# A diffusion block's second feed-forward network: first-matrix tiles in pairs of seven half-size products, mixed with the second matrix in eighths

## The chip, the core and the metric

The kernel runs on one core of a Trainium2 chip. The metric is device microseconds of an execution; the time before is the median of three runs. The engines are TensorE (PE, with its weight loads as PEld), VectorE (DVE), ScalarE (ACT), GpSimd (POOL) and SyncE (SP), which issues the transfers.

## What is computed

Two layers of a transformer block over 512 latent tokens of width 1024 (and 256 context tokens in layer 0): attention, LayerNorm, a squared-ReLU network of width 4096, LayerNorm. The change is in the network of layer 1:

```python
def sqrelu_mlp(h, w1, w2):
    return jnp.square(jax.nn.relu(h @ w1)) @ w2

x = layer_norm(alpha * x + g1 * ax, ln1_g[i], ln1_b[i])
fx = sqrelu_mlp(x * (1.0 + sc2) + sh2, mlp_w1[i], mlp_w2[i])
x = layer_norm(alpha * x + g2 * fx, ln2_g[i], ln2_b[i])
```

All is float32. A product is made of three passes: each operand is split in a high part (rounded to float32r) and the rest, and high x high, high x low and low x high are summed in PSUM.

## The kernel before

*Products and splits.* `mm3` (L321 to L324) issues the three matmuls of 128 x 128 x n. `wsplit` (L297 to L318) brings a 128 x 1024 weight tile: a transfer into `w_raw` (four buffers), the cast `w_h` on ScalarE (L264), the subtraction `w_l` on VectorE (L312). `w_h` and `w_l` have four buffers each (`NH`).

*The order.* TensorE's order is written out by generators that the class `Flow` runs with a planned clock: a `yield` names what must be done before the next matmuls are issued. The other engines' order is made by the framework's scheduler from the same program. Every engine works its queue in order.

*Layer 1's network, `mlp` with l = 1.* `ln_job` (L521 on) transposes a normalised token block of 128 on TensorE (`xn_t`, L532), ScalarE scales it into `hx_v` (two buffers that it shares with `g_tmp`), and two splits write `hx1m`. The hidden width has 32 tiles of 128. They are worked in four quarters of eight tiles: for each tile 8 x 3 matmuls of 512 columns (`h_ps`, a wide accumulator of which PSUM holds two; the weight is the stationary operand, the tokens stream), then `relu` on ScalarE, the square on GpSimd (in the first quarter on VectorE), the cast `hid` and its subtraction. Tiles 0 to 3 are done in two slices of 256 tokens, so that they can start before the last token blocks are ready. Then `tok_product` works the second matrix: for either half of the 1024 outputs and each of four token blocks a group of 24 matmuls of 512 columns (`y_ps`, one of four narrow accumulators), with four weight tiles for a half. The groups of quarter 0 are copied into `fx`, those of quarters 1 and 2 are added to it on VectorE; then `fx` is multiplied by the gate and added to `acc` on GpSimd. The last quarter goes straight through `gated_add` (L560 on): `g_tmp` on VectorE, the sum into `acc` (on GpSimd for half 0, on VectorE for half 1), the statistics `bn`.

*The end.* `done4` takes a block's moments, has GpSimd raise the variance to -1/2 (`rstd`), and VectorE does two passes of 1024 with `l2g` and `l2b`, then the block goes out. The last group of all is done in two slices of 256 outputs.

Of the kernel before, what the change touches and what calls it, by code (L numbers as in the profile page):

```python
# [234 lines left out]
def hybrid_block(ctx: ExitStack, tc: tile.TileContext, t: dict, out: bass.AP):  # L235
# [31 lines left out]
    def gp(us, deps, fn, lat=LAT, **kw):  # L267
        fn(**kw)  # L268
# [51 lines left out]

    def mm3(o, lh, ll, rh, rl, start, stop):  # L321
        nc.tensor.matmul(out=o, lhsT=lh, rhs=rh, start=start, stop=False)  # L322
        nc.tensor.matmul(out=o, lhsT=lh, rhs=rl, start=False, stop=False)  # L323
        last["pe"] = nc.tensor.matmul(out=o, lhsT=ll, rhs=rh, start=False, stop=stop)  # L324

# [194 lines left out]

    def ln_job(pool, acc, tb, hx, A, B, ready, st, dep):  # L521
        dep = normalise(acc, st, dep)
# [3 lines left out]
        for q in range(2):  # L526
            yield [dep, sm_.ok]
            pt = psm("xn_t")
            slot = sm_.take()
            for j in range(4):  # L530
                k = 4 * q + j
                nc.tensor.transpose(out=pt[:, j * P:(j + 1) * P], in_=acc[:, k * P:(k + 1) * P], identity=ident)  # L532
            p = fl.pe(4 * mm(128))
            v = pool.tile([P, 4, P], F32, name="hx_v", tag="tmp", bufs=2)
# [1148 lines left out]
```

## Time and profile before

| what | value |
| --- | --- |
| median of three runs | 1679.1 us (1677.09 to 1680.61) |
| span of the profiled execution | 1669.8 us |
| what lies around the span, by the median | 9.3 us |
| PE, PEld busy | 1609.0, 1387.8 us |
| DVE, ACT, POOL busy | 935.4, 669.1, 344.2 us |
| layer 1's network and the end | from 1297.5 us on |

The profile is one execution. A page gives busy time by engine, then the chain of work that ended last, then groups of instructions by line. A row of the timeline reads: start, duration, engine, line, operation, out<-in, shape, count, and in brackets the idle time before it with what ended it. Matmuls overlap, so a row's duration is more than its step: the time of a matmul in a row of them is the distance of starts. A row of a table by stretches reads: window, length, then busy time and count of PE, PEld, DVE, ACT and POOL, the granted clock of TensorE, the share of the transfer engines and their GB/s.

### The profile page before, as it was taken

To read this page: it belongs to the slowest core of one execution; us is meant where nothing else is said; L and a number is where in the kernel's file an instruction comes from. 1 tells how busy PE (TensorE), PEld (TensorE's weight loads), DVE (VectorE), ACT (ScalarE), POOL (GpSimd) and SP (SyncE) were. 2 spreads that over 40 slices of the span, in tenths; PEclk is the share of its full clock that TensorE was granted. 3 is DMA by queue.
4 is the path that set the end of the run, shared out by engine and by line. 5 is a ranking of instruction groups with operands and counts; after the bars stand their busy time and mean duration, and the time that the engine had idled before them with its cause. 6 is when DMAs were issued, how large, how long until landed. Compare 5 with 4: busy or idle time off the path is not lost.

```text
span 1669.8 us, 23525 instructions
## 1 busy us (share of the span) xinstructions
PE 1609.0 (96%) x9153; PEld 1387.8 (83%) x9153; DVE 935.4 (56%) x1717; ACT 669.1 (40%) x1377; POOL 344.2 (21%) x314
## 2 busy tenths in 40 slices
PE   7899999999999999999999999999989899999998
PEld 5787777789889889879978998999877888888886
DVE  4655677668845353344446777776757552332436
ACT  3465675363223113212316555555543533222231
POOL 1333454100002001342211122221000001113422
PEclk9999999999999999999999999999999999999999
DMA  9111550524443243344312122211133323232321
GB/s 371 41 51 33 178 177 28 195 81 160 142 161 127 88 147 131 101 126 139 114 54 101 51 71 72 66 45 39 48 114 116 105 94 105 73 115 76 114 89 51
DMA packets 57239, 174.77 MB, mean 105 GB/s; under 512 B 7144, under 2 KB 13096, under 8 KB 57128
## 3 DMA queue, kind: packets, MB, share of 16 engines
q1 hardware_dynamic: 57128, 173.27, 30.8%
q8 instruction: 72, 1.18, 0.3%
q14 instruction: 39, 0.32, 0.1%
HBM read 165.35 MB, written 7.90 MB: 104 GB/s over the span
## 4 chain that ended last, share of the span: by engine, by line
PE 76%; DVE 9%; issue 5%; ACT 4%; DMA 3%; POOL 3%; SPq 0%; DVEq 0%; POOLq 0%; ACTq 0%
PE y_ps L324 10%; PE y_ps L323 10%; PE y_ps L322 10%; PE h_ps L322 8%; PE h_ps L323 8%; PE h_ps L324 8%; PE qkv_ps L322 2%; PE qkv_ps L323 2%; PE qkv_ps L324 2%; PE o_ps L1060 2%; PE s_ps L1376 2%; PE pT_ps L1078 2%; DVE w_l L312 2%; PE o_ps L1414 1%; PE s_ps L1027 1%
## 5 line engine op out<-in xcount | busy, mean ns | idle before, releaser
L264 ACT CAST w_h<-w_raw 128x1024 fp32r<-128x1024 f32 (+1 forms) x185 | 186.6, 1015 | 406.6 <-PE y_ps L324 207.9
L312 DVE TENSOR_TENSOR w_l<-w_raw,w_h 128x1024 fp32r<-128x1024 f32 (+1 forms) x185 | 222.1, 1211 | 216.3 <-ACT w_h L264 215.9
L323 PE MATMUL y_ps<-w_l,hid 128*128 128x512 f32 (+1 forms) x648 | 254.2, 392 | 1.8 <-DVE w_l L312 1.7
L324 PE MATMUL y_ps<-w_h,hid 128*128 128x512 f32 (+1 forms) x648 | 254.2, 392 | 0.4 <-DVE hid L260 0.2
L322 PE MATMUL y_ps<-w_h,hid 128*128 128x512 f32 (+1 forms) x648 | 254.3, 392 | 0.0
L268 POOL TENSOR_TENSOR relu<-relu 128x768 f32<-128x768 f32 (+1 forms) x48 | 80.9, 1686 | 604.2 <-ACT relu L264 604.2
L324 PE MATMUL h_ps<-hx0m,w_l 128*128 128x384 f32 (+1 forms) x528 | 175.4, 332 | 1.2 <-DVE w_l L312 1.0
L322 PE MATMUL h_ps<-hx0m,w_h 128*128 128x384 f32 (+1 forms) x528 | 175.2, 332 | 0.0
L323 PE MATMUL h_ps<-hx0m,w_h 128*128 128x384 f32 (+1 forms) x528 | 174.9, 331 | 0.0
L323 PEld LDWEIGHTS y_ps<-w_l,hid 128*128 128x128 f32 x648 | 121.9, 188 | 30.9 <-DVE w_l L312 3.3
L324 PEld LDWEIGHTS y_ps<-w_h,hid 128*128 128x128 f32 x648 | 121.9, 188 | 29.5 <-DVE hid L260 1.8
L322 PEld LDWEIGHTS y_ps<-w_h,hid 128*128 128x128 f32 x648 | 122.0, 188 | 28.0
L322 PE MATMUL qkv_ps<-w_h,hx 128*128 128x384 f32 (+1 forms) x384 | 126.9, 331 | 0.1
L323 PE MATMUL qkv_ps<-w_l,hx 128*128 128x384 f32 (+1 forms) x384 | 122.4, 319 | 0.7 <-DVE w_l L312 0.7
L324 PE MATMUL qkv_ps<-w_h,hx 128*128 128x384 f32 (+1 forms) x384 | 122.1, 318 | 0.0
L268 POOL TENSOR_TENSOR e<-e,sm 128x512 f32<-128x512 f32 (+2 forms) x96 | 92.7, 978 | 109.7 <-DVE sm L260 90.5
L322 PE MATMUL h_ps<-hx1m,w_h 128*128 128x512 f32 (+1 forms) x288 | 107.7, 374 | 3.5 <-ACT relu L264 3.5
L323 PE MATMUL h_ps<-hx1m,w_h 128*128 128x512 f32 (+1 forms) x288 | 107.2, 372 | 0.0
L324 PE MATMUL h_ps<-hx1m,w_l 128*128 128x512 f32 (+1 forms) x288 | 107.1, 372 | 0.0
L324 PEld LDWEIGHTS h_ps<-hx0m,w_l 128*128 128x128 f32 x528 | 99.1, 188 | 2.4 <-DVE w_l L312 2.4
L322 PEld LDWEIGHTS h_ps<-hx0m,w_h 128*128 128x128 f32 x528 | 99.1, 188 | 0.2
L323 PEld LDWEIGHTS h_ps<-hx0m,w_h 128*128 128x128 f32 x528 | 99.1, 188 | 0.1
(226 smaller groups left out, 3092.3 us busy)
## 6 DMA issues: line engine op xcount, KB each, us to landing
w_raw<-in_w SPq DMA_DIRECT2D x128, 512.0 KB, 3.5
w_raw<-in_w_adaT SPq DMA_DIRECT2D x56, 512.0 KB, 3.5
w_raw<-in_w_ada SPq DMA_DIRECT2D x24, 512.0 KB, 4.4
w_raw<-in_b_w SPq DMA_DIRECT2D x32, 384.0 KB, 3.5
raw<-in_w_ada SPq DMA_DIRECT2D x16, 512.0 KB, 9.5
w_raw<-in_a_wq SPq DMA_DIRECT2D x8, 512.0 KB, 4.3
w_raw<-in_a_wo SPq DMA_DIRECT2D x8, 512.0 KB, 4.2
w_raw<-in_b_wo SPq DMA_DIRECT2D x8, 512.0 KB, 4.1
```

The lines of the kernel that those rows point to most:

```text
L264: fn(**kw)
L268: fn(**kw)
L312: last["split"] = nc.vector.tensor_tensor(**kw)
L322: nc.tensor.matmul(out=o, lhsT=lh, rhs=rh, start=start, stop=False)
L323: nc.tensor.matmul(out=o, lhsT=lh, rhs=rl, start=False, stop=False)
L324: last["pe"] = nc.tensor.matmul(out=o, lhsT=ll, rhs=rh, start=False, stop=stop)
L1027: nc.tensor.matmul(out=sp[:, 512:512 + CTX], lhsT=q_, rhs=kT[:, kvh, hl, SEQ:TOK], start=(hl == 0), stop=(hl == 1))
L1060: nc.tensor.matmul(out=po[odd * HD:odd * HD + HD, 0:256], lhsT=vv[:, kb, kvh], rhs=pt_[:, odd * 256:odd * 256 + 256], start=(i == 0), stop ...
L1078: nc.tensor.transpose(out=pp[:, c * P:(c + 1) * P], in_=es[j][:, i * P:(i + 1) * P], identity=ident)
L1376: nc.tensor.matmul(out=sp[:, c * 512:c * 512 + 384], lhsT=qTt[:, tt, hl, qb * P:(qb + 1) * P], rhs=kS[:, tt, c * 384:c * 384 + 384], start ...
L1414: nc.tensor.matmul(out=po[:, qp * 256:(qp + 1) * 256], lhsT=vt[:, kb, vl], rhs=pt_[:, pl, a * 256:a * 256 + 256], start=(kp == 0 and pl == ...
```

## The change

Layer 1's network gets a function of its own, `mlp_pipe`; layer 0 keeps `mlp`. In it:

- Hidden tiles 0 to 5 are done as before (`plain`).
- Tiles 6 to 31 are done in 13 pairs, q = 3 to 15. A pair and the tokens are cut in 2 x 2 blocks: A (two weight tiles by two halves of the inner 1024) and B (the halves of the inner 1024 by two halves of the tokens). By Strassen's method in Winograd's form seven products A11, A12, S2, S1, S3, A22, S4 of 4 x 3 matmuls of 256 columns give the four blocks for which eight were needed. GpSimd makes the sums of weight blocks (`part_sums`: `e3`, `e1`, `e2` and the last for S4); each of the seven is split into a tile `w_half` that holds both parts (four buffers).
- Sums and differences of token blocks are made once (`token_sums`: eight differences on GpSimd in place in `fx`, which keeps the transposed tokens, then splits into `T`).
- Three products sum up in one accumulator X: it is copied out by ScalarE (`a1`, `a2`, `a3`) before the next product adds to it. VectorE adds the other products from two narrow accumulators. ScalarE does relu and square.
- The second matrix goes in eighths: eight sets of 512 hidden values; a group is 12 matmuls of 512 columns (`y_half` twice), for half of the outputs and one token block, and `sink` sums into `fx`. Between the products of a pair four groups are put (`mix`), in pairs 14 and 15 four half groups. `ahead` asks for the next pair's first four half tiles and for two second-matrix tiles.
- `last_y` does what is left: two groups of the eighth 6 (half 1) left open in their accumulators, then the eighth 7: half 0, then half 1 with the open groups first; blocks 2 and 3 do both eighths' half 1.
- `bc` tiles have three buffers instead of four, `hx_v` is gone in layer 1.

The core of the diff:

```diff
-NRAW, NH = 3, 4
+NRAW, NH, NQ = 3, 4, 4
...
+    def mlp_pipe(l, hx, ready, apool, pool, late, ntok, acc, get_gates, done, res, fx, T):
...
+        def part_sums(q):
+            (a1, g1, f1), (a2, g2, f2) = raw_tile(), raw_tile()
...
+            yield half(a11, q1)
+            w12 = half(a12, q1)
+            yield w12
+            e3 = add(s3, a11, a21, ALU.subtract, [q1, q2])
+            e1 = add(a21, a21, a22, ALU.add, [e3])
+            e2 = add(s2, a21, a11, ALU.subtract, [e1])
+            yield half(s2, e2)
+            yield half(a21, e1)
+            yield half(s3, e3)
+            w = half(a22, q2)
...
+            w = half(a12, add(a12, a12, s2, ALU.subtract, [e2, w12.t]))
...
+        def product(o, w, b, start):
+            kw = {} if start else {"skip_group_check": True}
+            for kk in range(4):
+                c_ = slice(kk * P, (kk + 1) * P)
+                mm3(o, w.h[:, c_], w.l[:, c_], b(kk, 0), b(kk, 1), start and kk == 0, kk == 3, **kw)
...
+        def pair(q, mix, ahead):
...
+            p = product(X, A11, lower(t1, 0), True)
+            a1 = ac(nh, [p], nc.scalar.copy, out=r0[:, t1], in_=X)
...
+            p = product(y[:, 0:nh], A12, lower(t1, 4), True)
...
+            yield from mix()
+            yield [a1, S2.t, Tr[1]]
+            p = product(X, S2, whole(1), False)
+            a2 = ac(nh, [p], nc.scalar.copy, out=r0[:, t2], in_=X)
...
+            p5 = product(z, S1, whole(0), True)
+            yield from mix()
+            yield [a2, S3.t, Tr[2]]
+            p = product(X, S3, whole(2), False)
+            a3 = ac(nh, [p], nc.scalar.copy, out=r1[:, t2], in_=X)
+            d3 = dv(nh, [p5, a3], nc.vector.tensor_tensor, out=r1[:, t2], in0=z, in1=r1[:, t2], op=ALU.add)
+            ahead()
+            yield from mix()
+            yield [a3, A22.t, Tr[3]]
+            p = product(X, A22, whole(3), False)
...
+            yield [d3, S4.t]
+            p = product(z, S4, lower(t2, 4), False)
...
+            squared(q, 0, r0, [d], slice(0, ntok))
+            yield from mix()
...
+            early = []
+            y_weights(6, 1)
+            y_weights(7, 0)
...
+            y_weights(7, 1)
...
+        yield from plain(range(4), [slice(i, i + 256) for i in range(0, ntok, 256)], sums)
+        yield from plain((4, 5), [slice(0, ntok)])
...
+        for q in range(3, 16):
+            n = 2 if q < 14 else 1
...
+            yield from pair(q, steps(ys, n), ahead)
+        yield from steps(ys, 99)()
+        yield from last_y()
```

Three places of the built program. The first is ScalarE inside the network. Before, between tiles 2 and 4 of the second quarter, a weight tile's cast, a relu out of PSUM and a `hid` cast follow each other:

```order
L264 CAST w_h_13545<-w_raw_13544 128x1024 [waits DMAHW2_49,DVE_49,PE_49]
L264 ACTIVATE relu_13430<-h_ps_13399 128x512 [waits DVE_49,PE_49]
L264 CAST hid_13324<-relu_13430 128x512 [waits Pool_49]
L264 CAST w_h_13581<-w_raw_13580 128x1024 [waits DMAHW3_49,PE_49]
L264 ACTIVATE relu_13466<-h_ps_13435 128x512 [waits DVE_49,PE_49]
L264 CAST hid_13324<-relu_13466 128x512 [waits Pool_49]
```

Now, in pair 6 from its first product on (13732 is the accumulator X, 13733 and 13734 the two result tiles, 13721, 13724, 13728 the half tiles S3, A22, S4, 13835 the next pair's A11, 13857 the second weight tile of a later group):

```order
L264 CAST w_half_13721<-w_sum_13631 128x512 [waits PE_49]
L264 COPY relu_13733<-h_ps_13732 128x256
L264 CAST w_half_13724<-w_raw_13628 128x512 [waits PE_49]
L264 CAST w_h_13857<-w_raw_13856 128x1024 [waits DMAHW6_49]
L264 CAST w_half_13728<-w_raw_13627 128x512 [waits PE_49,Pool_49]
L264 COPY relu_13733<-h_ps_13732 128x256
L264 CAST w_half_13835<-w_raw_13830 128x512 [waits DMAHW4_49,DVE_49,PE_49]
L264 COPY relu_13734<-h_ps_13732 128x256 [waits DVE_49,PE_49]
L264 CAST w_half_13838<-w_raw_13830 128x512 [waits DVE_49]
L264 ACTIVATE relu_13734<-relu_13734 128x256 [waits DVE_49]
```

The copies of X, for which TensorE waits, stand behind casts of half tiles and, in one place, behind a cast that waits for a transfer.

The second is TensorE at the start of the last half of the second matrix. Before, the first group takes a new weight tile every six matmuls, four in all:

```order
L322 MATMUL y_ps_14897<-w_h_14874,hid_14437 128x512 [waits DVE_49,Activation_49]
L323 MATMUL y_ps_14897<-w_l_14875,hid_14437 128x512 [waits DVE_49]
L324 MATMUL y_ps_14897<-w_h_14874,hid_14437 128x512
L322 MATMUL y_ps_14897<-w_h_14874,hid_14437 128x512
L323 MATMUL y_ps_14897<-w_l_14875,hid_14437 128x512
L324 MATMUL y_ps_14897<-w_h_14874,hid_14437 128x512
L322 MATMUL y_ps_14897<-w_h_14880,hid_14438 128x512 [waits Activation_49]
```

Now it takes two (the eighth (7,1): 15792 and 15798, in the buffers in which (7,0) lay), and the accumulator 15693 holds the eighth 6 already:

```order
L325 MATMUL y_ps_15773<-w_l_15689,hid_15544 128x512
L326 MATMUL y_ps_15773<-w_h_15688,hid_15544 128x512
L324 MATMUL y_ps_15693<-w_h_15792,hid_15365 128x512 [waits Activation_49]
L325 MATMUL y_ps_15693<-w_l_15793,hid_15365 128x512 [waits DVE_49]
L326 MATMUL y_ps_15693<-w_h_15792,hid_15365 128x512
L324 MATMUL y_ps_15693<-w_h_15792,hid_15365 128x512
L325 MATMUL y_ps_15693<-w_l_15793,hid_15365 128x512
L326 MATMUL y_ps_15693<-w_h_15792,hid_15365 128x512
L324 MATMUL y_ps_15693<-w_h_15798,hid_15544 128x512 [waits Activation_49]
```

So the group that ends ahead of it is the one that frees the buffers of its weights.

The third is VectorE at the end, from block 2's product with its gate on (12407 is block 2, 12408 block 3). Before:

```order
L563 TENSOR_TENSOR g_tmp_15000<-y_ps_14975,g2x_14163 128x512 [waits PE_49]
L260 TENSOR_TENSOR acc1_12407<-acc1_12407,g_tmp_15000 128x512 [waits DVE_49]
L260 BN_STATS bn_14841<-acc1_12407 128x6 [waits DVE_49]
L260 BN_AGGR mv_15004<-bn_14841 128x2 [waits DVE_49]
L260 TENSOR_SCALAR rstd_15006<-mv_15004 128x1 [waits DVE_49]
L260 SCALAR_TENSOR_TENSOR acc1_12407<-acc1_12407,mv_15004,l2g_14926 128x1024
L260 TENSOR_TENSOR g_tmp_15037<-y_ps_15012,g2x_14163 128x256 [waits PE_49]
L260 SCALAR_TENSOR_TENSOR acc1_12407<-acc1_12407,rstd_15006,l2b_14928 128x1024 [waits DVE_49,Pool_49]
```

Now block 1's second wide pass (12406) stands behind block 2's first row:

```order
L568 TENSOR_TENSOR g_tmp_15880<-y_ps_15855,g2x_14533 128x512 [waits PE_49]
L260 SCALAR_TENSOR_TENSOR acc1_12406<-acc1_12406,rstd_15849,l2b_15821 128x1024 [waits DVE_49,Pool_49]
L260 TENSOR_TENSOR acc1_12407<-acc1_12407,g_tmp_15880 128x512 [waits DVE_49]
L260 BN_STATS bn_15771<-acc1_12407 128x6 [waits DVE_49]
L260 TENSOR_TENSOR g_tmp_15917<-y_ps_15892,g2x_14533 128x256 [waits PE_49]
L260 BN_AGGR mv_15884<-bn_15771 128x2 [waits DVE_49]
L260 TENSOR_TENSOR acc1_12408<-acc1_12408,g_tmp_15917 128x256 [waits DVE_49]
L260 TENSOR_SCALAR rstd_15886<-mv_15884 128x1 [waits DVE_49]
L260 SCALAR_TENSOR_TENSOR acc1_12407<-acc1_12407,mv_15884,l2g_15819 128x1024
L260 SCALAR_TENSOR_TENSOR acc1_12407<-acc1_12407,rstd_15886,l2b_15821 128x1024 [waits DVE_49,Pool_49]
```

The rows of three blocks interleave where before one block's were through when the next began.

More of the change, by code (lines that the diff above doesn't have):

```diff
@@ L319, in hybrid_block, with mm3 @@
     last = {}
[L321 to L324, printed above, removed]
+    def mm3(o, lh, ll, rh, rl, start, stop, **kw):
+        nc.tensor.matmul(out=o, lhsT=lh, rhs=rh, start=start, stop=False, **kw)
+        nc.tensor.matmul(out=o, lhsT=lh, rhs=rl, start=False, stop=False, **kw)
+        last["pe"] = nc.tensor.matmul(out=o, lhsT=ll, rhs=rh, start=False, stop=stop, **kw)
     cT = load_const("cT", [P, KT, 2])
@@ L490, in split, with bcast_load @@
         return a, dv(n, [a], nc.vector.tensor_tensor, lat=lat, out=lo, in0=src, in1=f(hi), op=ALU.subtract)
-    def bcast_load(pool, src, nm, c0=0):
-        b = pool.tile([P, D], F32, name=nm, tag="bc", bufs=BC)
+    def bcast_load(pool, src, nm, c0=0, n=BC):
+        b = pool.tile([P, D], F32, name=nm, tag="bc", bufs=n)
         reload(b, src, c0)
@@ L518, in normalise, with ln_job @@
         return fl.op("D", dve(620), [d], LNLAT)
-    def ln_job(pool, acc, tb, hx, A, B, ready, st, dep):
+    def ln_job(pool, acc, tb, hx, A, B, ready, st, dep, keep=None):
         dep = normalise(acc, st, dep)
@@ L533, in ln_job @@
             p = fl.pe(4 * mm(128))
-            v = pool.tile([P, 4, P], F32, name="hx_v", tag="tmp", bufs=2)
+            if keep is not None:
+                v = keep.rearrange("p (k t) -> p k t", t=P)[:, 4 * q:4 * q + 4]
+            else:
+                v = pool.tile([P, 4, P], F32, name="hx_v", tag="tmp", bufs=2)
             for j in range(4):
@@ L1573, in hybrid_block @@
         queue["split"] = last["split"].ins.name
-        lb = bcast_load(pool, lnrow[1, 1:2], "l1b")
+        lb = bcast_load(pool, lnrow[1, 1:2], "l1b", 0, 3)
         scale_inplace(lb, ALPHA)
         A, B = affine(1, 0, 1, 1, 3, 4, "m1", 1)
-        hx = hx_big("hx1m", SEQ)
+        b = big("hx1m")
+        hx = [b[:, q * 2048:q * 2048 + 2048].rearrange("p (k h t) -> p k h t", k=2, h=2) for q in range(4)]
+        T = [b[:, 8192 + q * 2048:10240 + q * 2048] for q in range(2)]
+        T = T + [pool.tile([P, 2048], F32R, name="hx_sum", tag="T", bufs=2) for _ in range(2)]
+        T = [x.rearrange("p (k h t) -> p k h t", k=4, h=2) for x in T]
+        fx = [pool.tile([P, D], F32, name="fx", tag="fx", bufs=NXB) for _ in range(NXB)]
         ready = [NO] * NXB
         def done3(tb, st, r):
-            fl.add(ln_job(pool, acc[tb], tb, hx, A, B, ready, st, r), 0)
+            fl.add(ln_job(pool, acc[tb], tb, hx, A, B, ready, st, r, fx[tb]), 0)
         def done4(tb, st, r):
             if tb == 0:
-                st2["g"] = bcast_load(pool, lnrow[1, 2:3], "l2g")
-                st2["b"] = bcast_load(pool, lnrow[1, 3:4], "l2b")
+                st2["g"] = bcast_load(pool, lnrow[1, 2:3], "l2g", 0, 3)
+                st2["b"] = bcast_load(pool, lnrow[1, 3:4], "l2b", 0, 3)
             mv, rstd, d = moments(st, r)
@@ L1597, in g2b @@
         def g2b():
-            yield
-            return [bcast_load(pool, gate_d[(1, 5)][0:1], "g2x")]
+            return [bcast_load(pool, gate_d[(1, 5)][0:1], "g2x", 0, 3)]
         def main1():
@@ L1607, in main1 @@
             res = [lambda tb=tb: residual(acc[tb], gx, lb, last["pe"]) for tb in range(NXB)]
-            yield from mlp(1, hx, ready, apool, pool, SEQ, acc, g2b, done4, None, res)
+            yield from mlp_pipe(1, hx, ready, apool, pool, late, SEQ, acc, g2b, done4, res, fx, T)
         fl.add(main1(), 2)
```

229 lines of the change are left out of this document (227 added, 2 removed).

## The prediction

> **What bounds the kernel now.** I read the page first, then the table by stretches for the last 370 us (layer 1's feed-forward network and the end), then TensorE's waits there, then single rows.
>
> ```profile
> span 1669.8 us, 23525 instructions
> PE 76%; DVE 9%; issue 5%; ACT 4%; DMA 3%; POOL 3%; SPq 0%; DVEq 0%; POOLq 0%; ACTq 0%
> ```
>
> The chain that ended last is three quarters TensorE. The table by stretches (busy us of PE, PEld, DVE, ACT, POOL, then the granted clock) shows the stage that is changed:
>
> ```profile
> 1297.50:1302.00 4.50, 4.50 (x23) 4.50 (x22) 3.78 (x8) 4.50 (x15) 0.00 (x0) 0.52 0.87 273
> 1304.00:1330.00 26.00, 22.45 (x173) 21.32 (x172) 10.28 (x14) 9.90 (x17) 0.00 (x0) 1.00 0.20 65
> 1400.00:1500.00 100.00, 100.00 (x431) 80.38 (x430) 33.89 (x36) 29.28 (x38) 15.83 (x10) 1.00 0.29 95
> 1500.00:1600.00 100.00, 100.00 (x431) 80.70 (x430) 35.43 (x36) 29.53 (x38) 38.35 (x26) 1.00 0.29 95
> 1655.00:1669.80 14.80, 6.93 (x54) 6.50 (x52) 11.24 (x19) 0.00 (x0) 2.51 (x2) 0.91 0.27 106
> ```
>
> From 1330 on TensorE never pauses, at full clock; VectorE is busy 35 of 100 us, ScalarE 30, GpSimd 16 to 38. So here time is matmuls times their step, and the other engines have room. Two pauses stand ahead of that, and the rows at the edges give the step of a 512-column matmul, with the count of a grouping by form (three lines of each kind):
>
> ```profile
> 1315.23 0.39 PE L322 MATMUL h_ps<-hx1m,w_h 128*128 128x256 f32 x1 [1.52 <-ACT relu L264]
> 1323.19 0.39 PE L322 MATMUL h_ps<-hx1m,w_h 128*128 128x256 f32 x1 [2.03 <-ACT relu L264]
> 1326.10 0.39 PE L322 MATMUL h_ps<-hx1m,w_h 128*128 128x512 f32 x1
> 1656.09 0.28 PE L322 MATMUL y_ps<-w_h,hid 128*128 128x256 f32 x1
> ...
> L323 PE MATMUL y_ps<-w_l,hid 128*128 128x512 f32 x248 | 97.9, 395 | 0.0
> L322 PE MATMUL h_ps<-hx1m,w_h 128*128 128x512 f32 x224 | 88.5, 395 | 0.0
> ```
>
> 3 x (248 + 224) = 1416 matmuls from 1326.10 to 1656.09: 330.0 / 1416 = 0.2330 us each. For 256 columns the early slices of the same stage serve:
>
> ```profile
> 1304.80 0.28 PE L322 MATMUL h_ps<-hx1m,w_h 128*128 128x256 f32 x1
> 1313.44 0.27 PE L324 MATMUL h_ps<-hx1m,w_l 128*128 128x256 f32 x1
> ...
> L323 PE MATMUL h_ps<-hx1m,w_h 128*128 128x256 f32 x26 | 7.3, 279 | 0.0
> L324 PE MATMUL h_ps<-hx1m,w_l 128*128 128x256 f32 x26 | 7.3, 279 | 0.0
> L322 PE MATMUL h_ps<-hx1m,w_h 128*128 128x256 f32 x25 | 7.0, 279 | 0.0
> ```
>
> The groups are those from 1304.75 to 1313.5; two of their 77 had begun earlier, so 74 steps lie between the two rows: 8.64 / 74 = 0.1168 us, half of 0.2330, although each has its own weight load.
>
> **The change part by part.** *The products.* Thirteen pairs (tiles 6 to 31) go from 2 x 8 x 3 = 48 matmuls of 512 columns to 7 x 4 x 3 = 84 of 256. 624 x 0.2330 = 145.4 us go, 1092 x 0.1168 = 127.5 come: **-17.9 us**, all on the path. (The built program has 468 rows more on TensorE: 1092 - 624.)
>
> The Trainium skill, "TensorE: Matmul & The Clock Gate", section "Back-to-back issue gap", gives an isolated gap of N/2.4 + 2.5 ns; by it the two steps would be 0.2158 and 0.1092 us and the gain 15.4 us. No step here is that short, so the rows decide.
>
> *What a pair asks of the other engines.* Their durations:
>
> ```profile
> L264 ACT CAST w_h<-w_raw 128x1024 fp32r<-128x1024 f32 x68 | 71.4, 1050 | 176.7 <-PE y_ps L324 108.1 <-PE h_ps L323 68.6
> L312 DVE TENSOR_TENSOR w_l<-w_raw,w_h 128x1024 fp32r<-128x1024 f32 x68 | 84.3, 1246 | 102.8 <-ACT w_h L264 102.8
> L264 ACT CAST hid<-relu 128x512 fp32r<-128x512 f32 x32 | 19.9, 620 | 50.5 <-POOL relu L268 40.7 <-DVE relu L260 9.9
> L260 DVE TENSOR_TENSOR hid<-relu,hid 128x512 fp32r<-128x512 f32 x32 | 22.2, 692 | 42.9 <-ACT hid L264 42.9
> L264 ACT CAST hx1m<-hx_v 128x256 fp32r<-128x256 f32 x16 | 6.0, 453 | 0.0
> L260 DVE TENSOR_TENSOR hx1m<-hx_v,hx1m 128x256 fp32r<-128x256 f32 x16 | 6.1, 419 | 3.0 <-ACT hx1m L264 3.0
> L268 POOL TENSOR_TENSOR relu<-relu 128x512 f32<-128x512 f32 x24 | 38.0, 1584 | 241.0 <-ACT relu L264 241.0
> ```
>
> A product takes 12 x 0.1168 = 1.40 us, a group of the second matrix 12 x 0.2330 = 2.80, a pair 7 x 1.40 + 4 x 2.80 = 21.0. In that time ScalarE has 7 half-tile casts (0.62), 2 full ones (1.05), 5 copies or relus of 256 (0.45) and 5 passes of 512 (0.62): 11.8 us; VectorE 7 half-tile subtractions, 4 sums into fx and 2 hid splits (0.69), 2 full subtractions (1.25) and 3 adds of 256 (0.42): 12.7; GpSimd 4 x 1.58 = 6.3. Each fits, so only order can hold TensorE up. From a pair's start, with ScalarE's and VectorE's rows as the order lists them: S2 needs A11's copy at 5.6 and it is there at 1.40 + 0.62 (S3's cast ahead of it) + 0.45 = 2.5; S3 needs S2's copy at 11.2, there at 7.0 + 0.62 + 0.45 = 8.1; A22 needs S3's copy at 15.4, there at 13.1; S4 needs the add behind it at 16.8, there at 13.5. The tightest is the pair's last hid: after S4 (18.2) ScalarE's queue holds 0.62 + 0.62 + 0.62 + 1.05 by 21.1, VectorE then the full subtraction (22.4), a sum into fx and the split (23.7); the next pair's first group reads it at 21.0 + 2.80 + 1.40 = 25.2, 1.5 us later. So I book nothing for waits inside pairs. In pairs 14 and 15 half a group covers S3's copy: 1.40 against 0.45, still free. Below nothing no reason is seen; above, the rivals give the price. The second matrix keeps its matmuls, and the transfers are the same 64 tiles of 512 KB. That its sums into fx double, and that the squares move from GpSimd (24 x 1.58) to ScalarE, is counted above.
>
> *The start.* Until tile 6 the matmuls stay the same. Added are 8 GpSimd differences with 8 casts and 8 splits; the casts stand ahead of tile 0's relu on ScalarE, for which tile 1 waits today (the 1.52 us above). Against that hx_v loses its shared buffer, and the fourth block's transposes move behind tile 0's first slice:
>
> ```profile
> 1295.20 1.51 ACT L264 ACTIVATE hx_v<-xn_t,Bm,Am 128x128 f32<-128x128 f32 x4 [0.94 <-DVE hx1m L260]
> 1296.76 1.12 PE L532 MATMUL xn_t<-identr,acc 128*128 128x128 f32 x4 [0.76 <-ACT hx_v L264]
> 1298.10 0.41 PE L324 MATMUL h_ps<-hx1m,w_l 128*128 128x256 f32 x1
> 1298.31 0.41 PE L322 MATMUL h_ps<-hx1m,w_h 128*128 128x256 f32 x1
> ```
>
> Gain: at most 0.94 + 0.76. The differences can start with the third block's hx_v, about 1297, 2 us behind the second block's row at 1295.20. At 8 x 1.58 they are through at 1309.6, before tile 0 ends (1313.44); at 8 x 2.20 (below) only at 1314.6, and with a cast behind them they keep the relu some 2 us. I take **-0.7**, ends -1.7 and +3.
>
> *The last weights.* The tiles of the eighth (7,1) go into the buffers of (7,0), which TensorE releases in its last group: at T - 1.4 and T, if T is that group's end. Before, four tiles came free one by one, the first 4.2 us ahead of T. Rows that follow:
>
> ```profile
> 1629.05 1.30 POOL L268 TENSOR_TENSOR acc<-acc,g_tmp 128x512 f32<-128x512 f32 x1 [4.30 <-DVE g_tmp L563]
> 1641.08 2.20 POOL L268 TENSOR_TENSOR acc<-acc,g_tmp 128x512 f32<-128x512 f32 x1 [5.13 <-DVE g_tmp L563]
> 1656.28 0.69 DVE L563 TENSOR_TENSOR g_tmp<-y_ps,g2x 128x512 f32<-128x512 f32 x1
> 1658.78 1.28 DVE L260 SCALAR_TENSOR_TENSOR acc<-acc,mv,l2g 128x1024 f32<-128x1024 f32 x1
> 1661.66 0.28 PE L324 MATMUL y_ps<-w_h,hid 128*128 128x256 f32 x1
> 1662.04 0.42 DVE L260 TENSOR_TENSOR g_tmp<-y_ps,g2x 128x256 f32<-128x256 f32 x1
> ```
>
> The first cast ends at T - 0.3; VectorE first finishes the third block (0.69, GpSimd's sum of 1.30 to 2.20, 0.69 of statistics: T + 0.1 to T + 1.0), then subtracts 1.25; TensorE's second matmul wants it at T + 0.23: 1.1 to 2.0 us lost. The second cast ends at T + 1.15, its subtraction follows a product of 0.69 at about T + 3.2, wanted at T + 2.7: 0.5. **+1.6**, ends 0 and 2.5.
>
> *The tail.* The last four blocks need 12, 12, 24 and 24 matmuls' time; before it was 24 each. VectorE's work for a block starts at its g_tmp and reaches the first wide multiply after 2.50 us (1656.28 to 1658.78); with two wide ones of 1.28 that is 5.1, for three blocks 15.2, and 0.8 for the fourth's first half: 16.0 us. From the first block's end to the last matmul are 5 x 2.80 = 14.0. Today the last g_tmp starts right behind the last matmul (1661.66, 1662.04); after the change it finds VectorE 2.0 us behind, or 2.4 where the fourth block's statistics of half 0 come in first (half of 0.69). **+2.2**, ends 0 and 3.
>
> Sum: -17.9 - 0.7 + 1.6 + 2.2 = **-14.8 us**. The profiled execution's span goes from 1669.8 to 1655.0; the shown runs' median, 1679.1, lies 9.3 above the span, and I leave that as it is: **1664.3**.
>
> **The rivals.** *Nothing is lost at the end* (weights and VectorE keep up): -17.9 - 0.7, 1660.5. For it: VectorE is free for 65 of 100 us ahead of the end; against: its queue is in order, and what lies behind the last group can't be done early.
>
> *Pairs wait a little*, at the last hid, where 1.5 us of slack are worked out with rows that have VectorE 35% busy and would have it 60%: at 0.5 us a pair +6.5, 1670.8.
>
> *Slower: the second weight tile of a pair.* It shares its raw buffer with the first, so its transfer goes out only after that one's subtraction, 1.4 us into the next pair, and its cast stands ahead of S4's cast and S2's copy on ScalarE. Two groups of transfers of the same size:
>
> ```profile
> w_raw<-in_w SPq DMA_DIRECT2D x128, 512.0 KB, 3.5
> raw<-in_w_ada SPq DMA_DIRECT2D x16, 512.0 KB, 9.5
> ```
>
> With 3.5 us it is cast by 6.0, ahead of S2's end at 7.0. With 9.5 the copy ends at 1.4 + 9.5 + 1.05 + 0.62 + 0.45 = 13.0, S3 wanted it at 11.2: 1.8 us in each of 11 pairs, +19.8, 1684.1. It decides from a landing time of 7.7 us on, and the kernel gets slower from about 9. Against it: the queue's share is 0.29 in these stretches.
>
> *The clock falls.* Where TensorE paused often, around 1297, the clock was 0.52 and a 256-column step 0.21 us (the rows 1298.10 and 1298.31), for that stretch's 23 matmuls; a single 1.52 or 2.03 us left it at 1.00. If each pair had a pause long enough, 2.1 + 23 x (0.21 - 0.117) = 4.2 us a pair, 55 in all: -14.8 + 55 = +40, 1719. It needs the turn-round of the accumulator to fail by over 2 us. The Trainium skill, "TensorE: Matmul & The Clock Gate", section "Why this matters for your kernels", warns of matmuls thinner than 512 and of pauses over some 3 us, behind which the clock swings. This trace has 256-column runs at full clock.
>
> **How the numbers follow.** Forecast 0.70 (own range 1661 to 1668), nothing lost at the end 0.08, pairs wait a little 0.13, the raw buffer 0.06, the clock 0.03. A measurement tells 0.2%, 3.4 us. Faster by more: the first three but for the upper end of the third, 0.88; within: 0.05, from that end and short landings of the fourth; slower: 0.07. The range 1659 to 1673 holds the first three with the bounds of start and end, and leaves out some 0.13.
>
> **What would show it.** Right: 1092 matmuls of 256 columns at 0.117 between tiles 6 and 31, no wait of TensorE inside pairs, two short waits on w_l at the start of the last quarter-block, and the last g_tmp about 2 us behind the last matmul. Wrong: a wait that returns every 21 us on hid, w_half or the accumulator, a granted clock under 1.00, or a start that is over 3 us longer.

## The result, and the profile after

The changed kernel takes **1669.4 us** (median of 4 runs, 1667.0 to 1670.0) where the kernel before takes 1679.6 beside it (4 runs): ratio 0.9941, 95% interval 0.9927 to 0.9956, about 10 us faster. A second measurement gave 1670.0 (6 runs) against 1676.4 (11 runs), ratio 0.9962 (0.9947 to 0.9976). The prediction said 1664.3, faster, with a range of 1659 to 1673: the sign and the range hold, but 5 us of the 14.8 are missing, and the time lies outside the forecast's own range of 1661 to 1668.

The page of the changed kernel, its span and the shares of the chain that ended last (before: span 1669.8, PE 76%, DVE 9%, ACT 4%):

```profile
span 1665.1 us, 24866 instructions
...
PE 74%; DVE 10%; ACT 5%; issue 5%; DMA 3%; POOL 3%; SPq 0%; DVEq 0%; POOLq 0%; ACTq 0%
```

The two spans differ by 4.7 us, half of what the runs differ by. So the stage that is changed needs a mark of its own: the third group of transposes of the normalised rows (xn_t), the one that waits 0.9 us for a cast of hx1m. It is the same work in both kernels, just ahead of the first matrix. Its row before:

```profile
1289.60 0.63 PE L532 MATMUL xn_t<-identr,acc 128*128 128x128 f32 x4 [0.91 <-ACT hx1m L264]
```

The changed kernel: first its mark, then TensorE's waits from tile 1 on (start, length, engine, line, operation, and in brackets the idle time ahead with its releaser), with the rows beside them and the last matmul:

```profile
1293.51 0.63 PE L534 MATMUL xn_t<-identr,acc 128*128 128x128 f32 x4 [0.92 <-ACT hx1m L264]
...
1315.63 0.28 PE L326 MATMUL h_ps<-hx1m,w_l 128*128 128x256 f32 x1
1319.23 0.38 PE L324 MATMUL h_ps<-hx1m,w_h 128*128 128x256 f32 x1 [3.32 <-ACT relu L264]
...
1320.08 0.41 PE L326 MATMUL h_ps<-hx1m,w_l 128*128 128x256 f32 x1
1320.29 0.41 PE L324 MATMUL h_ps<-hx1m,w_h 128*128 128x256 f32 x1
...
1328.71 0.39 PE L324 MATMUL h_ps<-hx1m,w_h 128*128 128x256 f32 x1 [2.03 <-ACT relu L264]
...
1332.99 0.57 PE L324 MATMUL h_ps<-hx1m,w_h 128*128 128x512 f32 x1
...
1355.50 0.29 PE L324 MATMUL h_ps<-hx1m,w_half 128*128 128x256 f32 x1
...
1566.57 0.29 PE L324 MATMUL h_ps<-hx1m,w_half 128*128 128x256 f32 x1
...
1596.56 0.39 PE L324 MATMUL h_ps<-hx_sum,w_half 128*128 128x256 f32 x1 [0.24 <-ACT relu L264]
...
1603.70 0.28 PE L324 MATMUL h_ps<-hx1m,w_half 128*128 128x256 f32 x1
...
1609.12 0.39 PE L324 MATMUL h_ps<-hx1m,w_half 128*128 128x256 f32 x1 [1.03 <-ACT relu L264]
...
1637.27 0.40 PE L324 MATMUL y_ps<-w_h,hid 128*128 128x512 f32 x1
1638.64 0.50 PE L325 MATMUL y_ps<-w_l,hid 128*128 128x512 f32 x1 [0.97 <-DVE w_l L313]
...
1639.91 0.40 PE L324 MATMUL y_ps<-w_h,hid 128*128 128x512 f32 x1
1640.38 0.50 PE L325 MATMUL y_ps<-w_l,hid 128*128 128x512 f32 x1
...
1655.65 0.28 PE L326 MATMUL y_ps<-w_h,hid 128*128 128x256 f32 x1
```

From the mark to the end of the span are 1669.8 - 1289.6 = 380.2 us before and 1665.1 - 1293.5 = 371.6 after: the stage gained 8.6 us. The mark itself came 3.9 us later in this execution; the experiments show how much of that is chance. The rows give the rest: the pause ahead of tile 1 has grown from 1.52 to 3.32 us, behind it a 256-column step takes 0.21 us (1320.08 to 1320.29), and the first 512-column step comes 39.5 us behind the mark (before 36.5). In the pairs nothing waits until the last two: 1355.50 and 1566.57 are the first matmuls of pairs 3 and 13, ten pairs in 211.07 us, 21.11 each. Pairs 14 and 15 wait once each (pair 15 begins at 1603.70), and w_l is waited for near the end.

The table by stretches (busy us of PE, PEld, DVE, ACT, POOL, granted clock) answers to that of before, where VectorE had 34 to 35 of 100 us, ScalarE 29, and the start ran at a clock of 1.00:

```profile
1315.00:1333.00 18.00, 12.65 (x81) 12.24 (x81) 13.86 (x17) 8.54 (x13) 5.22 (x4) 0.82 0.27 88
...
1400.00:1500.00 100.00, 100.00 (x626) 89.88 (x626) 60.39 (x85) 47.46 (x87) 30.27 (x20) 1.00 0.33 106
1500.00:1600.00 100.00, 99.76 (x629) 89.58 (x628) 66.97 (x88) 51.90 (x94) 36.87 (x25) 1.00 0.31 98
```

The clock is 0.82 in the start and 1.00 in the pairs; VectorE is at 60 to 67%, as worked out ahead, and TensorE is still never kept waiting there, but for the 0.24 us at 1596.56.

That wait and the next (1609.12) end with a copy of X on ScalarE. What held ScalarE's queue ahead of these copies stands in its own rows and in one of GpSimd's:

```profile
1594.67 1.05 ACT L264 CAST w_h<-w_raw 128x1024 fp32r<-128x1024 f32 x1 [3.35 <-DMA w_raw<-in_w]
1599.37 1.68 POOL L268 TENSOR_TENSOR w_sum<-w_raw 128x512 f32<-128x512 f32 x1 [4.25 <-DMA w_raw<-in_w]
1603.83 0.62 ACT L264 CAST w_half<-w_sum 128x512 fp32r<-128x512 f32 x1 [4.26 <-POOL w_sum L268]
1608.70 0.36 ACT L264 COPY relu<-h_ps 128x256 f32<-128x256 f32 x1
```

In pair 14 the queue stood 3.35 us for a transfer, with S2's copy behind it. For pair 15 GpSimd's sum waited 4.25 us for a transfer, ScalarE's cast of that sum waited 4.26 us for GpSimd, and A11's copy came at 1608.70 behind all that had gathered in the queue.

Why tile 0's relu is late, first in the view of one tile (count, least, median and longest ns, first and last start; fx, then the first difference alone, then hx_sum, which gets half of the splits), then in ScalarE's timeline:

```profile
L268 POOL TENSOR_TENSOR fx<-fx x8: 1357/1532/5352, 1300.9 to 1315.5; 128x512 f32<-128x512 f32 x8
...
L268 POOL TENSOR_TENSOR fx<-fx x1: 5352/5352/5352, 1300.9 to 1300.9; 128x512 f32<-128x512 f32 x1
...
L264 ACT CAST hx_sum<-fx x4: 617/622/656, 1308.8 to 1317.1; 128x512 fp32r<-128x512 f32 x4
L260 DVE TENSOR_TENSOR hx_sum<-fx,hx_sum x4: 678/1213/1778, 1312.5 to 1319.4; 128x512 fp32r<-128x512 f32 x4
```

```profile
1317.12 0.62 ACT L264 CAST hx_sum<-fx 128x512 fp32r<-128x512 f32 x1 [1.05 <-POOL fx L268]
1317.64 1.04 ACT L264 CAST w_h<-w_raw 128x1024 fp32r<-128x1024 f32 x1
1318.59 0.59 ACT L264 ACTIVATE relu<-h_ps 128x512 f32<-128x512 f32 x1
```

GpSimd's eight differences run from 1300.9 to 1317.1: the first takes 5.35 us, the median is 1.53, the average 2.0. VectorE's splits run at the same time, and those take up to 1.78 us instead of 0.68. In the kernel start_order below, which moves the splits of 512 columns away, the last three differences take 1.29 us each. Tile 0's matmuls end at 1315.63; its relu stands in ScalarE's queue behind the last cast of a difference and a cast of 1.04, and starts at 1318.59. The Trainium skill, "SBUF — State Buffer", section "Who interferes with whom", says that a VectorE instruction with two inputs in SBUF and a GpSimd instruction that reads SBUF hold each other up, the later one waiting for the earlier; the trace agrees, 0.68 against 1.78.

The last blocks on VectorE, the first block's g_tmp and the last one:

```profile
1642.11 0.68 DVE L568 TENSOR_TENSOR g_tmp<-y_ps,g2x 128x512 f32<-128x512 f32 x1
...
1657.42 0.42 DVE L260 TENSOR_TENSOR g_tmp<-y_ps,g2x 128x256 f32<-128x256 f32 x1
```

The last g_tmp starts 1.8 us behind the last matmul (1655.65); before it was 0.4.

### The profile page after: what moved, and what is told of

Same layout as the page of the kernel before. It is cut to its first block, busy times and chain, and to the rows that moved or that the text cites. A ratio compares the mean times of both kernels' runs of the same rounds, so it can differ in the third digit from the quotient of the medians.

```text
span 1665.1 us, 24866 instructions
## 1 busy us (share of the span) xinstructions
PE 1599.0 (96%) x9621; PEld 1405.1 (84%) x9621; DVE 1029.5 (62%) x1855; ACT 726.2 (44%) x1528; POOL 401.6 (24%) x350
## 4 chain that ended last, share of the span: by engine, by line
PE 74%; DVE 10%; ACT 5%; issue 5%; DMA 3%; POOL 3%; SPq 0%; DVEq 0%; POOLq 0%; ACTq 0%
PE y_ps L326 9%; PE y_ps L325 9%; PE y_ps L324 9%; PE h_ps L324 8%; PE h_ps L325 7%; PE h_ps L326 7%; PE qkv_ps L324 2%; PE qkv_ps L325 2%; PE qkv_ps L326 2%; PE o_ps L1369 2%; PE pT_ps L1387 2%; PE s_ps L1685 2%; DVE w_l L313 2%; PE o_ps L1723 1%; DMA w_raw<-in_w 1%
## 5 line engine op out<-in xcount | busy, mean ns | idle before, releaser
L264 ACT CAST w_h<-w_raw 128x1024 fp32r<-128x1024 f32 (+1 forms) x159 | 159.1, 1007 | 293.2 <-PE y_ps L326 136.2
L313 DVE TENSOR_TENSOR w_l<-w_raw,w_h 128x1024 fp32r<-128x1024 f32 (+1 forms) x159 | 192.0, 1217 | 153.2 <-ACT w_h L264 152.9
L268 POOL TENSOR_TENSOR relu<-relu 128x768 f32<-128x768 f32 x24 | 42.0, 1751 | 366.4 <-ACT relu L264 366.4
L260 DVE CUSTOM_DVE_ANT_0 w_raw<-w_raw,cB 128x1024 f32<-128x1024 f32 x56 | 79.4, 1420 | 25.3 <-DMA w_raw<-in_w_adaT 24.9
L260 DVE TENSOR_TENSOR fx<-y_ps,fx 128x512 f32<-128x512 f32 x68 | 46.7, 687 | 77.0 <-PE y_ps L326 77.0
L268 POOL TENSOR_TENSOR rope<-rope,rope 128x256 f32<-128x256 f32 (+1 forms) x40 | 33.8, 845 | 216.1 <-DVE rope L260 174.9
```

The source lines that it names most:

```text
L313: last["split"] = nc.vector.tensor_tensor(**kw)
```

## The experiments

All times here are from the mark, in the profile of each kernel; the last column is from the last matmul to the last g_tmp. Two profiles of the same kernel agree to 0.3 us by this measure, so it tells more than the runs, which scatter by 4 us and more. Of before_again, swap, tail_order and mix15 there is one execution each, so these four are read from the mark alone.

| kernel | first 512-column step | last matmul | end of span | lag of g_tmp |
|---|---|---|---|---|
| before | 36.5 | 372.1 | 380.2 | 0.4 |
| before_again | 36.8 | 372.4 | 380.5 | 0.3 |
| changed | 39.5 | 362.1 | 371.6 | 1.8 |
| after_again | 39.5 | 362.1 | 371.6 | 1.8 |
| start_order | 36.1 | 359.0 | 368.5 | 1.8 |
| start_vector | 33.4 | 355.9 | 365.7 | 1.8 |
| swap | 32.5 | 355.1 | 364.6 | 1.8 |
| own_tiles | 38.9 | 359.7 | 369.1 | 1.7 |
| tail_order | 39.5 | 360.1 | 368.9 | 1.0 |
| mix15 | 39.5 | 361.0 | 370.5 | 1.8 |
| classic | 39.5 | 377.5 | 387.3 | 1.8 |
| all_four | 33.2 | 352.6 | 361.4 | 0.8 |
| all_five | 30.5 | 350.0 | 358.9 | 0.8 |

**Both kernels once more.** No edit.

> The changed kernel once more, as the yardstick for the three others. Theory: its gain on before is the 8.6 us that the two profiles show from the third xn_t group on, give or take the 4 us by which the earlier stages differ between two executions: 1669.4, ratio 0.995. Rival (the earlier stages differ because of the change, not by chance): the span up to the third xn_t group is again 4 us longer than before's.

> The kernel before, profiled once more. Theory (the stages ahead of the third xn_t group vary from execution to execution, by up to 7 us in the profiles of the changed kernel and its variants, and the first profile of before was an early one): again 380.2 us from that group to the end, the group itself anywhere from 1289 to 1300, and 1.9 us between the span and the run's time. Rival (the changed kernel is later at that group because of the change): the group at 1289.6 again, within 1 us.

Both repeat their stage, 371.6 and 380.5. The mark, in the order of the rows: before a second time, the changed kernel a second time, and the earliest of its variants (swap).

```profile
1292.85 0.63 PE L532 MATMUL xn_t<-identr,acc 128*128 128x128 f32 x4 [0.90 <-ACT hx1m L264]
```

```profile
1299.61 0.63 PE L534 MATMUL xn_t<-identr,acc 128*128 128x128 f32 x4 [0.96 <-ACT hx1m L264]
```

```profile
1290.80 0.63 PE L534 MATMUL xn_t<-identr,acc 128*128 128x128 f32 x4 [0.91 <-ACT hx1m L264]
```

Before has it at 1289.6 and 1292.9, so the rival that this place is fixed falls; the changed kernel and its variants have it anywhere from 1290.8 to 1299.6. The stages ahead of the change scatter, and a single pair of spans says nothing below some 5 us. The granted clock is probably a part of this: between 100 us and the mark the two earliest (before, swap) have one stretch of 3.4 us at half clock each, the latest (after_again) 20.5 us in all. Whether the changed kernel is later there on average stays open; two marks of before are too few. Between span and time lie 1.8 us in both (1673.3 and 1675.1; 1671.2 and 1673.0), not the 9.3 us that the prediction let stand "around" it. With 1.8 us the first profiled execution of before took 1671.6, less than any measured run of that kernel (the lowest is 1672.5), so it was probably just a quick one; its own time is not known.

**The products alone.** Every pair with the eight ordinary half-products:

```
-            A11, A12, S2, S1, S3, A22, S4 = Wp[q]
+            A11, A12, A21, A22 = Wp[q]
...
+            for fi, u, v in ((0, A11, A12), (1, A21, A22)):
+                for n, w in enumerate((u, v)):
+                    for kk in range(4):
+                        mm3(X[:, cs_], w.h[:, c_], w.l[:, c_], hxs(hx, 4 * n + kk, 0, slice(0, ntok)), ...)
```

> The 13 pairs with 8 half-products of 512 columns each (48 matmuls, four half-tiles of weights, no weight sums on GpSimd) instead of 7 of 256 tokens (84 matmuls); the token sums are still made, and nothing reads them. Start, mixing with the second matrix and the end stay. Theory (the gain is the matmul count alone, at 0.2330 and 0.1183 us a step): 145.4 - 129.2 = 16.2 us slower than the changed kernel, less up to 1.8 for the waits of pairs 14 and 15 if these go: 386.0 to 387.8 us from the third xn_t group to the end (changed kernel 371.6), 1684 to 1686, slower than before. Rival (the mixing, or keeping fx in place, brings part of the gain): 8 to 12 us slower than the changed kernel, level with before.

It takes 1682.1 us, ratio to before 1.0031 (1.0018 to 1.0045): slower than before, as the theory has it, and 15.7 us behind the changed kernel from the mark. The first matmuls of pairs 3 and 13 in its timeline:

```profile
1355.57 0.40 PE L324 MATMUL h_ps<-hx1m,w_half 128*128 128x512 f32 x1
...
1579.81 0.40 PE L324 MATMUL h_ps<-hx1m,w_half 128*128 128x512 f32 x1
```

Ten pairs take 224.24 us, 22.42 each, against 21.11 with seven products: 1.32 us a pair, 17.1 in thirteen, of which the waits of pairs 14 and 15 (which this kernel hasn't) give 1.8 back. The rival, that mixing the two matrices brings part of the gain, falls: without the seven products the new order of the work makes the stage 7 us longer than before, of which the losses at the start and the end are 5.8 (3.0, 1.4 and 1.4 in the table of the next section), so nothing is left that the mixing could have won.

**The start: order, engine, and cover.** Three kernels change only what stands between the normalised rows and the first 512-column step. First, the casts of the sums are tied behind tile 3's relu in ScalarE's queue, and with them go the splits on VectorE:

```
+        def late_cast(**kw):
+            tc.add_manual_dep(nc.scalar.copy(**kw).ins, last["relu"], ORDER, reason="queue order")
...
-                    Tr[i].append(split(512, d[0], o, T[i][:, :, 0, tok], T[i][:, :, 1, tok])[1])
+                    a = ac(512, d, late_cast, out=hi, in_=o)
+                    Tr[i].append(dv(512, [a], nc.vector.tensor_tensor, out=lo, in0=o, in1=f(hi), op=ALU.subtract))
```

> The 8 casts of the token sums stand behind tile 3's relu on ScalarE; GpSimd's differences stay where they are. Theory A (the casts' place ahead of tile 0's relu is what the start lost): the pause before tile 1 falls from 3.32 to about 1.5 us, the 256-column steps of 0.21 us behind it (some 28 of them, 2.9 us) are gone: 4.7 us less than the changed kernel, 1664.7. Rival B (GpSimd's differences slow VectorE's splits beside them, 1.36 us for 256 columns instead of 0.41, and the clock falls at this place whatever the order is): under 1 us.

TensorE's two pauses and the first 512-column step:

```profile
1319.38 0.38 PE L324 MATMUL h_ps<-hx1m,w_h 128*128 128x256 f32 x1 [1.52 <-ACT relu L775]
...
1327.34 0.38 PE L324 MATMUL h_ps<-hx1m,w_h 128*128 128x256 f32 x1 [2.04 <-ACT relu L775]
...
1331.79 0.40 PE L324 MATMUL h_ps<-hx1m,w_h 128*128 128x512 f32 x1
```

The pause ahead of tile 1 is again that of before, and the slow steps behind it are gone; but the second pause is still followed by 16 slow steps. From the mark it won 3.1 us of the 4.7 expected; its runs: 1667.1, ratio 0.9943 (0.9931 to 0.9955). Rival B, under 1 us, falls; so does the part of theory A that one order would mend both stretches. This kernel takes the casts and the splits out of the way together, so it doesn't tell the two apart.

Second, the differences on VectorE:

```
-                    d = [gp(pool2(512), d, nc.gpsimd.tensor_tensor, out=o, in0=u, in1=v, op=ALU.subtract)]
+                    d = [dv(512, d, nc.vector.tensor_tensor, out=o, in0=u, in1=v, op=ALU.subtract)]
```

> The 8 differences run on VectorE instead of GpSimd, the casts stay ahead of tile 0's relu. Theory A: 8 x 0.69 = 5.5 us of VectorE, the casts are through long before tile 0 ends, so pause and cold steps go as in the other kernel: 4.7 us less, 1664.7; the splits beside them take 0.41 (256 columns) and 0.69 (512) instead of 1.36 and 1.78. Rival B (what costs is that GpSimd runs beside VectorE): this kernel gains the 4.7, the one with the other order does not. Rival C (VectorE's queue, 5.5 us longer, now holds tile 1's w_l up): the pause stays, with w_l as its releaser, and under 1 us is won.

The view of the tile fx and the two pauses:

```profile
L260 DVE TENSOR_TENSOR fx<-fx x8: 681/686/694, 1304.7 to 1314.6; 128x512 f32<-128x512 f32 x8
...
L260 DVE TENSOR_TENSOR hx_sum<-fx,hx_sum x4: 685/688/692, 1309.6 to 1316.0; 128x512 fp32r<-128x512 f32 x4
```

```profile
1316.50 0.39 PE L324 MATMUL h_ps<-hx1m,w_h 128*128 128x256 f32 x1 [0.69 <-ACT relu L264]
...
1323.73 0.38 PE L324 MATMUL h_ps<-hx1m,w_h 128*128 128x256 f32 x1 [1.36 <-ACT relu L264]
```

Eight differences take 0.69 us each and no split is held up (0.69, where it was up to 1.78). From the mark it won 5.9 us, more than the 4.7; its runs: 1661.3, ratio 0.9919 (0.9905 to 0.9933). The pauses are even shorter than before the change, since the relu now also stands ahead of the 1.04 us cast of w_h, and no slow step is left. Rival C, VectorE as the new holder, falls, and so does B as it is put here, since the other order did win a part.

Third, the order of the tiles in the second slice:

```
-                for ft in fts:
+                for ft in fts if n == 0 else (0, 2, 1, 3):
```

> The changed kernel, but in the second slice of tiles 0 to 3 the order is 0, 2, 1, 3, so that TensorE works on tile 2's 24 matmuls (2.8 us) while tile 0's relu is awaited. Theory (it is the pause that brings the slow steps): the pauses shrink from 3.3 and 2.0 us to under 0.8, and the two stretches of 14 to 17 slow steps (1.6 and 1.5 us) go: first 512-column step of the first matrix at 31.4 us instead of 39.5, 363.5 us to the end. Rival (the clock falls at this place by itself, or from what the other engines do): the pauses go, the slow stretches stay, 366.6 us.

```profile
1316.61 0.39 PE L324 MATMUL h_ps<-hx1m,w_h 128*128 128x256 f32 x1 [0.58 <-ACT relu L264]
...
1320.36 0.39 PE L324 MATMUL h_ps<-hx1m,w_h 128*128 128x256 f32 x1 [0.68 <-ACT relu L264]
...
1323.27 0.44 PE L324 MATMUL h_ps<-hx1m,w_h 128*128 128x512 f32 x1
```

With the casts and GpSimd's differences as they were, only covered by tile 2's matmuls, both pauses shrink to under 0.7 us and no slow stretch follows: 7.0 us less than the changed kernel (8.1 expected). So the slow steps come from the pause, not from the place or from the other engines. (The first step behind any pause is long by some 0.1 us, here too.)

**The last weights.** (7,1) gets tiles of its own and is asked for ahead of (7,0)'s groups:

```
+                if (c, half) == (7, 1):
+                    own = [pool.tile([P, 2048], F32R, name="w_own", tag="T", bufs=2) for _ in range(2)]
+                    hl = [[x[:, 0:1024], x[:, 1024:2048], None, None] for x in own]
```

> The two tiles of the last weights (7,1) are split into the buffers of the third and fourth token sum, free since pair 15's A22, instead of those of (7,0), and are loaded ahead of (7,0)'s groups. Theory: the two waits for w_l at the start of the last quarter-block (gaps of 1.37 and 0.47 us, 1.5 beyond a step) go: 1.5 us less than the changed kernel, 1667.9; the last g_tmp stays 1.8 us behind the last matmul, since VectorE's 15.3 us from the first of the last four blocks on move along. Rival (VectorE's backlog, not TensorE, sets the end): the waits go and the last g_tmp is 3.2 us behind the last matmul, no gain.

Both waits are gone. From the mark it is 2.5 us ahead of the changed kernel, of which 0.6 lie in its start (ScalarE's order there came out a little otherwise); the other 1.9 lie behind pair 15, 1.5 expected. The lag of g_tmp stays, so the rival falls. Its runs: 1666.6, ratio 0.9942 (0.9929 to 0.9955).

**The end.** With the same tiles, the groups of (7,0) and (7,1) alternate:

```
-            for tb in range(ntb):
+            for half, tb in ((0, 0), (0, 1), (1, 0), (0, 2), (1, 1), (0, 3), (1, 2), (1, 3)):
```

> The kernel with own tiles for the last weights, and in the last stage the groups of (7,0) and (7,1) alternate, so that the first two blocks end 5.6 and 2.8 us earlier against the last matmul. Theory (VectorE's queue of three block ends is what trails): the last g_tmp starts 0.4 us behind the last matmul instead of 1.8: 1.4 us less than with own tiles alone, 367.7 us from the third xn_t group to the end if the start is the same. Rival (the trailing work is the last block's own chain): the lag stays, 369.1.

```profile
1655.67 0.42 DVE L260 TENSOR_TENSOR g_tmp<-y_ps,g2x 128x256 f32<-128x256 f32 x1
...
1657.73 0.42 DVE L260 TENSOR_TENSOR g_tmp<-y_ps,g2x 128x256 f32<-128x256 f32 x1
```

The lag falls from 1.7 to 1.0, not to 0.4 (last matmul at 1656.69), and the time from the last matmul to the end from 9.4 to 8.8. Half of the expected gain: the queue of block ends was a part of the lag; what holds the rest is not settled.

**Pairs 14 and 15.** Pair 15's half-groups as 2, 1, 1, 0:

```
-            n = 2 if q < 14 else 1
+            n = [2] * 4 if q < 14 else [1] * 4 if q < 15 else [2, 1, 1, 0]
```

> Pair 15 takes its four half-groups as 2, 1, 1, 0 instead of 1, 1, 1, 1, so 2.8 us instead of 1.4 lie between A12 and S2. Theory (ScalarE's queue still holds the pair before's relu and cast ahead of A11's copy, half a group is too short a cover): the wait of 1.03 us (gap 1.42, and 0.1 of slow steps) ahead of S2 goes, 1.3 us less than the changed kernel, 370.3 us from the third xn_t group to the end. Rival (the copy is late by more than that, or the wait moves to A22, behind one half-group fewer): under 0.5 us.

TensorE's one wait in pairs 14 and 15:

```profile
1598.51 0.39 PE L324 MATMUL h_ps<-hx_sum,w_half 128*128 128x256 f32 x1 [0.32 <-ACT relu L264]
```

It is pair 14's, ahead of S3; the 1.03 us ahead of pair 15's S2 are gone, and the stage is 1.1 us shorter (1.3 expected), as the theory has it. More cover hides the late copy; it doesn't make it earlier.

**Together.**

> Differences on VectorE, own tiles for the last weights, the alternating end and pair 15's half-groups together. If the four losses are separate places, they add: 371.6 - 6.0 - 1.9 - 1.4 - 1.3 = 361.0 us from the third xn_t group to the end, some 10.6 us less than the changed kernel, 1659, ratio to before 0.989. Rival (they share a cover, above all VectorE, which gets the differences): under 8 us.

> The kernel with the four mends, and the order 0, 2, 1, 3 as well. Theory: its two pauses (gaps of 0.96 and 1.70 us) go, 2.4 us less than with four: 358.9 us from the third xn_t group to the end, 1654.8, ratio to before 0.9865. Rival (the relu of the next tiles comes late instead, since ScalarE's casts of the next weights stand ahead of it): no gain, 361.4.

The four take 361.4 us from the mark (361.0 expected): they add, to 0.4 us. The runs: **1657.2 us**, ratio to before 0.9879 (0.9859 to 0.9899), where the changed kernel has 0.9941 and 0.9962. With the order of the tiles as well it is 358.9, as expected, and 1656.4 us, ratio 0.9887 (0.9867 to 0.9907); the runs don't tell these two apart. Both beat both kernels.

## Why the prediction was right, and where it was short

The stage from the mark, term by term, predicted and measured:

| term | predicted | measured | from |
|---|---|---|---|
| products | -17.9 | -16.4 | 145.4 less 1092 x 0.1181 |
| start | -0.7 | +3.0 | 39.5 less 36.5 |
| waits in pairs | 0 | +1.8 | pairs 14 and 15: gaps of 0.64 and 1.42 less two steps, and a long first step behind each |
| last weights | +1.6 | +1.4 | gaps of 1.37 and 0.47 less two steps (1.9 by the kernel with own tiles) |
| tail | +2.2 | +1.4 | 9.5 less 8.1 |
| sum | -14.8 | -8.8 | read: 371.6 less 380.2 to 380.5, -8.6 to -8.9 |

*Products.* The mechanism is right and carries the result. The size was off by 1.5 us: a pair of 21.11 us leaves (21.11 - 48 x 0.2330) / 84 = 0.1181 us for a 256-column step, not the 0.1168 of the 74 steps of the start. Why is open; in the ten pairs from 1355.50 on the steps beside a busy GpSimd average 0.1184 us (181 of them) and the others 0.1182 (619), so it is not GpSimd. By the kernel with ordinary products the same term is 17.1, since its own 512-column steps, in short runs, come to 22.42 / 96 = 0.2336.

*Start.* This is the step that failed. "I take -0.7, ends -1.7 and +3": it came out at the upper end. The range named the mechanism (differences at 2.2 us, "with a cast behind them they keep the relu some 2 us"), and the choice fell on the other side of it, although the row with 2.20 us was the one with VectorE at work beside GpSimd, as here. The differences took 2.0 us on average, by the first one's 5.35: eight at the median of 1.53 would have been through at about 1313 (an estimate, 1300.9 + 8 x 1.53), ahead of tile 0's end. The gain at the other end came as well: tile 0's matmuls end 22.1 us behind the mark (1315.63) where they ended 23.8 behind it before (1313.44). Then the pause gives 1.8 back, and the two slow stretches, 17 and 15 steps, take 1.6 and 1.5 us more than such steps do at full clock. These were missing altogether: the clock stood among the rivals as something that the pairs might do, and was not asked of the one pause that the term itself made longer. They are 3.1 of the 3.7 us by which the term is off. The prediction had taken from before's profile that a pause of 2.03 us leaves the clock at 1.00; that was luck of the place where the pause fell, as the last section shows.

*Waits in pairs.* Right for eleven pairs, at VectorE loads of 60 to 67%; wrong for the last two. "In pairs 14 and 15 half a group covers S3's copy: 1.40 against 0.45, still free" set the copy's own time against the cover, but not what is ahead of it in ScalarE's queue, which for the full pairs had been counted. There stood casts that wait for a transfer or for GpSimd's sum (the four rows above): A11's copy began 5.0 us into pair 15 (1603.70 to 1608.70), where the prediction had it done at 2.5. With one half-group more ahead of S2 the 1.03 us go.

*Last weights* right in place and size. *Tail* right in place, 0.8 us too large: VectorE needed 15.3 us (1642.11 to 1657.42) where 16.0 were worked out.

*Around the span.* The 9.3 us between span and median were no constant of the run: 1.8 lie around the span, and the rest is that the profiled execution was quicker than the measured runs. The forecast, a difference taken off the median, was not harmed by it; a reader of the two spans alone would have seen half the gain.

Of the rivals, the raw buffer did not come up as it was put: the transfers took 3.5 us again, and in the full pairs nothing waited. But its path, a cast ahead of the copy in ScalarE's queue that waits for a transfer, is the one on which pair 14 waited, where half a group covers it. The clock did fall, but at two places in the start and not in the pairs; a granted clock under 1.00 was one of the prediction's own signs of being wrong.

So the sign came out right by the mechanism, the seven products. The sum is 6.0 us off, and that the time still lies in the range is due to the wide upper end, in which +3 for the start was counted; the 1.8 us of the last two pairs were in no term, and it was luck that the tail came out 0.8 us better than booked.

## What to carry to other kernels

Where a change puts new work ahead of an instruction that TensorE already waits for, price the pause by the slow end of the new work's rows (two engines on the same memory at once), and then price what the clock does behind a longer pause (here some 1.5 us each time that it fell). Cover counts from the end of the queue that the awaited instruction stands in, not from its own length. And a stage of a long kernel is best measured from a mark inside the trace: here it repeats to 0.3 us, while runs of the same kernel differ by 8.

## What the runs showed of the hardware

*Pauses and the clock.* Once TensorE ran at full clock (from some 15 us behind the mark), no slow stretch followed a pause of 0.6 to 1.6 us in any profile. Pauses of 3.3 and 3.4 us were followed by 14 to 17 slow steps (some 1.5 us lost) each time, in six profiles. Pauses of 2.03 or 2.04 us were followed by as many in six profiles, the changed kernel's among them, and by none in the two of before. The Trainium skill, "TensorE: Matmul & The Clock Gate", section "Why this matters for your kernels", puts the limit at some 3 us of idle time; here 2.0 us was enough in six of eight profiles, so the measurement decides, and the limit lies lower.

What decides at 2.0 us can be read from the granted clock: in these profiles it changes only at the edges of a grid of 3.41 us. The rows are stretches of this grid (length, PE's busy time and count, granted clock, transfers), two of the changed kernel and then two of before:

```profile
1326.54:1329.95 3.41, 1.38 (x12) 1.00 0.51 154
1329.95:1333.37 3.42, 3.42 (x17) 0.50 0.47 158
...
1318.85:1322.26 3.41, 2.31 (x20) 1.00 0.23 52
1322.26:1325.67 3.41, 2.48 (x21) 1.00 0.60 220
```

In the changed kernel the second pause lies whole in one stretch, where TensorE is idle for 2.03 of 3.41 us, and the next stretch runs at half clock. In before an edge divides the same pause into 1.10 and 0.93 us, and the clock stays. All thirteen profiles fit this between 1305 and 1640 us: behind each of the twelve stretches at full clock with 2.03 us or more of idle time comes one at half clock, and behind none of those with 1.62 or less. So what counts is the idle time within one stretch, and the limit lies between these two figures; a pause of 2.0 us can go either way, by where it falls. No run moved a pause along the grid on purpose.

*Two halves of one accumulator.* Tile 1's matmuls write the other half of the accumulator that tile 0's relu reads, and still wait for that relu; the order 0, 2, 1, 3 shortens the wait from 3.32 to 0.58 us without touching the data. Whether the chip or the framework asks for this wait, no run here shows.

*GpSimd beside VectorE.* A difference of 512 columns takes 2.0 us on average on GpSimd beside VectorE's splits (1.36 to 5.35), and these go from 0.68 up to 1.78; on GpSimd with VectorE idle it takes 1.29 (the last ones of start_order), on VectorE 0.69, and the splits then stay at 0.69.
